# The first eleven Strassen products of the retention input stage put into a fixed order, with the weight and operand sums rearranged to match

## The chip, the cores and the metric

The kernel runs on one NeuronCore of one Trainium2 chip. The metric is the device time of one execution in microseconds, the median of several. The five engines run their own instruction lists and meet at semaphores: TensorE (PE, with weight loads listed apart as PEld), VectorE (DVE), ScalarE (ACT), GpSimd (POOL) and SyncE (SP), whose queue issues most of the DMAs.

## The reference, cut to what matters

One step of a two-layer encoder trunk over 1024 prompt frames and 32 sample frames (T = 1056 columns in all, feature dimension D = 1024), in fp32. The part that the change touches is the input of the first layer, the retention mixer:

```python
h = rmsnorm(x, norm_mix[0])
proj = h @ w_in                     # w_in: 1024 x (2*1024 + 2*2048)
q, k, v, g = jnp.split(proj, [RET_QK, 2 * RET_QK, 2 * RET_QK + RET_V], axis=-1)
# q and k are rotated (rotary), g goes through silu, v into the recurrence
```

The kernel reaches nearly fp32 precision out of fast matmuls: each operand is split into a high part (a cast, on ACT) and a low part (operand minus high part, on DVE), and one product is the sum of high x high, high x low and low x high.

## The kernel before, in words

`ret_in` (line 799) makes q, k and the gates g of the retention layer. The 1056 columns are cut into four quarters c = 0 to 3 of TH = 264. It has two stages.

**The opening.** Head 0's q and k are made in the plain way: `plain(j, c, ds)` (line 918) runs 24 matmuls for each 128 rows (j = 0 is q, j = 1 is k, `ds` are its two row blocks) on quarter c, and a copy on ACT brings the result from PSUM to `qk0`. Quarters 0 and 1 run on operands that aren't normalised yet (`loose`, line 863). Meanwhile `root` (line 886) makes the norms' square roots, `row` (line 898) spreads them along the columns with three small matmuls and a copy, and `parts(c, after)` (line 911) scales a quarter of x, splits it in four pairs (`pair`, line 841: for c = 1 a scaling on ACT and a multiply on DVE; for the others two scalings on DVE; then the cast on ACT at line 856 and the subtraction on DVE at line 858) and leaves it in `XP`. PE's last plain products, of quarters 2 and 3, cover `parts(3)` and `parts(1)`.

**The products by Strassen's scheme.** All other outputs are made in units of 256 rows (`units`, line 954: gate units "g" and q/k units by turns), and for each half s of the columns (s = 0: quarters 0 and 1, s = 1: quarters 2 and 3) a unit takes seven products in place of eight. `product(f, s, i)` (line 443) is the i-th product of unit f on half s in the order `ORD` = M1, M2, M6, M5, M7, M4, M3; it is four k tiles of three matmuls (lines 459, 463, 464), twelve in all. M1, M6 and M7 share one PSUM bank (M6 adds onto M1), M2 and M4 a second, M5 and M3 a third. `snap` (line 436, the copy of line 438) brings a bank to SBUF on ACT before the next product writes on it, and `put` (line 967, the addition of line 968) makes an output block of 264 columns on DVE from a snapped copy and a bank. There are eight banks in all (line 809).

M1 and M2 need the plain split of the weights `rg` (`wgh`, `wgl`) and plain quarters of x. M6, M5, M7, M4 and M3 need sums: of weights, made from `rg` and `rv` by `weight_steps` (line 355; `wsh`/`wsl`, `wth`/`wtl`, `wv`), and of quarters of x, made by `x_sums` (line 323), each a subtraction of 128x1056 on DVE (line 336; s12, s22, s11, s21 in the change), a cast on ACT (line 331) and a subtraction on DVE (line 332), which together are named x5, x6, x7 and x4 after the product that reads them. X[0]'s operands of M6, M7 and M4 go to the tile `XC`, those of half 1 to `XD`, which takes the memory of the raw quarter 0 when that is done with.

What sets the order: each engine runs its list strictly as the framework's planner wrote it. The planner goes by the order in which the program issues instructions and by its own estimate of when each is ready, so products can be interleaved matmul by matmul. `order(a, b)` (line 75) puts instruction a behind b in the planner's list and adds no semaphore. Before, the order of the products comes from the sorted list `seq` (line 1072), which only sets in what order they are issued. The unit's weights are loaded by SP's queue (line 371), the first ones behind the last constant (`normed`, line 1055). On DVE the first gate split and the sums all come behind the last subtraction of `parts(1)` (`held_back`, line 1063).

Of the kernel before, what the change touches and what calls it, by code (L numbers as in the profile page):

```python
# [10 lines left out]
F32 = mybir.dt.float32  # L11
# [7 lines left out]
D = 1024  # L19
# [32 lines left out]
def trunk_kernel(ctx: ExitStack, tc: tile.TileContext, io):  # L52
# [295 lines left out]
    def seven(X, wsrc, sm, snap_room, begin, put, first):  # L348
        W, unit = {}, {}
# [85 lines left out]

        def snap(b):
            t = snap_room()
            ins = S.copy(t, b)  # L438
            if snap_after[0] is not None:
                order(ins, snap_after[0])  # L440
            return t

        def product(f, s, i, after):
# [42 lines left out]
        return weight_sums, product, weight_steps  # L486
# [312 lines left out]
    def ret_in(XP, qk_tile, cs, decays):  # L799
# [41 lines left out]
        def pair(kt, c, after):  # L841
# [44 lines left out]
        def root(c, xms=None, behind=None):  # L886
# [8 lines left out]
            V.tensor_scalar(m_, m_, 1.0 / D, EPS, op0=ALU.mult, op1=ALU.add)  # L895
            rsqrt(r_, t_, m_)

# [13 lines left out]
        def parts(c, after):  # L911
            for kt in range(0, KT, 2):
                end = pair(kt, c, after)
            return end
# [3 lines left out]
        def plain(j, c, ds=(0, 1), after=None):  # L918

            for d in ds:  # L920
# [14 lines left out]
                else:  # L935
                    order(S.copy(qk0[c][:, j, d], ps), last_r[0] or loosened[0])
# [57 lines left out]
        weight_sums, product, weight_steps = seven(X, wsrc, sm, lambda: room("sn"), begin, put, {})  # L994
# [47 lines left out]
        root(3, None, last_r[0])  # L1042
# [18 lines left out]
        first_sums = sums(0)  # L1061
        start = first_sums[0]
        first_sums[0] = lambda: held_back(start(), end[1])
        weight_sums(0, None, first_sums)
        for f in last:
            f()
        for f in sums(1):
            order(f(), x_end[0])
# [3 lines left out]
        seq = [(9.15 if k == 6 else k if k < 9 else max(k, 11 + 0.78 * (k - 9)), 0, k) for k in range(n)]  # L1072
        seq += [(max(k + 3.5, 8.5 + 0.6 * k), 1, k) for k in range(n)]
        for _, s, k in sorted(seq):
            f, i = divmod(k, 7)
            if s == 0 and i == 2 and f == 0:
                second = weight_steps(1, None, None, True)
                next(second)
            elif s == 0 and i == 2 and f + 1 < len(units):
# [1177 lines left out]
    def ffn_up(l, X, fc, sm, he, ready):  # L2257
# [25 lines left out]
        weight_sums, product, weight_steps = seven(X, lambda f: (io["w_up"][l, f], io["w_up"][l, NF + f]), sm,  # L2283
# [428 lines left out]
```

## Time and profile before

| what | value |
|---|---|
| median of 3 runs | 2736.07 us (2733.41 to 2737.28) |
| profiled execution, its own time | 2735.83 us |
| its span, first to last instruction | 2733.8 us |
| PE, DVE, ACT, POOL busy | 99%, 75%, 51%, 15% of the span |
| mean granted clock of PE | 0.997 of full speed |

The change works in the first 110 us of the span, mostly between 38 and 90 us. Times below are microseconds from the span's start unless marked ns. A row of the timeline gives the start, the length, the engine, the source line, the operation with output and inputs, the shapes, and in brackets how long the engine had been idle and what ended that. Neighbouring instructions overlap by some tens of nanoseconds, so the step from one start to the next is what an instruction costs in a full list.

### The profile page before, as it was taken

The numbers are of one execution on the slowest core, as the hardware profiler recorded it, in microseconds if no ns is written. First come the engines' busy times: TensorE is split into PE (matmuls) and PEld (weight loads), VectorE is DVE, ScalarE is ACT, GpSimd is POOL, SyncE is SP. The second block draws the span as 40 slices with busy tenths as digits, with TensorE's granted clock in tenths as the row PEclk, the third lists the DMA queues.
The fourth block names the chain that finished last, engine by engine and source line by source line (L and its number), as shares of the span: only waits on it lengthen the run. The fifth ranks groups of instructions, "written<-read, shape, count | busy, mean of one in ns | idle before, by whom it ended". The sixth has DMA issues, their size and how long they took to land. (4 is left out here: it accounts for less than half of the span.)

```text
span 2733.8 us, 55846 instructions
## 1 busy us (share of the span) xinstructions
PE 2713.2 (99%) x22416; PEld 2624.8 (96%) x22416; DVE 2055.0 (75%) x3645; ACT 1385.3 (51%) x2601; POOL 408.6 (15%) x671
## 2 busy tenths in 40 slices
PE   9999999999999999999999999999999999999998
PEld 9999987778999999999999999999999999999998
DVE  7876667776556988888876788785479888888766
ACT  7544354544345544444544567774355444446445
POOL 0000000000112211111221233320132111112113
PEclk9999999999999999999999999999999999999999
DMA  6233355544876234223888611116533433329884
GB/s 240 92 110 110 114 168 154 158 136 115 277 246 237 99 130 153 96 91 110 271 229 212 185 48 54 54 55 207 190 124 99 147 134 103 106 87 289 233 213 124
DMA packets 278307, 410.18 MB, mean 150 GB/s; under 512 B 57040, under 2 KB 206944, under 8 KB 273952
## 3 DMA queue, kind: packets, MB, share of 16 engines
q1 hardware_dynamic: 259616, 348.23, 38.9%
q0 software_dynamic: 18144, 57.85, 9.0%
q8 instruction: 175, 2.87, 0.4%
q14 instruction: 84, 0.69, 0.1%
q10 hardware_dynamic: 288, 0.54, 0.1%
HBM read 264.34 MB, written 142.21 MB: 149 GB/s over the span
## 5 line engine op out<-in xcount | busy, mean ns | idle before, releaser
L438 ACT COPY HR<-pu 128x264 f32<-128x264 f32 x264 | 98.6, 374 | 265.2 <-PE pu L464 259.5
L459 PE MATMUL pu<-XA,wgh 128*128 128x264 f32 x752 | 213.6, 284 | 0.1
L464 PE MATMUL pu<-XA,wgl 128*128 128x264 f32 x752 | 213.6, 284 | 0.0
L463 PE MATMUL pu<-XA,wgh 128*128 128x264 f32 x752 | 213.3, 284 | 0.0
L2294 DVE SCALAR_TENSOR_TENSOR AR<-AR,cw 128x1058 f32<-128x1058 f32 x88 | 116.0, 1320 | 71.5 <-ACT AR L2293 66.8
L2267 DVE TENSOR_TENSOR AR<-HR,pu 128x264 f32<-128x264 f32 (+2 forms) x440 | 144.7, 371 | 5.3 <-ACT HR L438 3.3
L459 PEld LDWEIGHTS pu<-XA,wgh 128*128 128x128 f32 x752 | 141.9, 189 | 0.4 <-ACT wgh L391 0.4
L463 PEld LDWEIGHTS pu<-XA,wgh 128*128 128x128 f32 x752 | 141.9, 189 | 0.0
L464 PEld LDWEIGHTS pu<-XA,wgl 128*128 128x128 f32 x752 | 141.5, 188 | 0.0
L2291 POOL COPY cst<-AR 128x2 f32<-128x2 f32 x88 | 51.4, 585 | 562.4 <-DVE AR L2267 562.4
L459 PE MATMUL pu<-XA,wth 128*128 128x264 f32 x464 | 132.3, 285 | 2.8 <-ACT wth L391 2.8
L459 PE MATMUL pu<-XA,wsh 128*128 128x264 f32 x464 | 132.2, 285 | 1.0 <-ACT HR L438 0.2
L464 PE MATMUL pu<-XA,wtl 128*128 128x264 f32 x464 | 132.4, 285 | 0.0
L464 PE MATMUL pu<-XA,wsl 128*128 128x264 f32 x464 | 131.8, 284 | 0.0
L463 PE MATMUL pu<-XA,wth 128*128 128x264 f32 x464 | 131.7, 284 | 0.0
L463 PE MATMUL pu<-XA,wsh 128*128 128x264 f32 x464 | 131.4, 283 | 0.0
L2295 DVE SCALAR_TENSOR_TENSOR AR<-AR,cw 128x1058 f32<-128x1058 f32 x88 | 115.9, 1319 | 0.0
L2293 ACT ACTIVATE AR<-AR,cw 128x1058 f32<-128x1058 f32 x88 | 111.8, 1272 | 7.5 <-DVE AR L2267 6.4
L392 DVE TENSOR_TENSOR wtl<-rv,wth 128x1024 fp32r<-128x1024 f32 x58 | 71.0, 1224 | 44.8 <-ACT wth L391 44.7
L391 ACT CAST wgh<-rg 128x1024 fp32r<-128x1024 f32 x58 | 61.0, 1051 | 81.1 <-PE pu L464 77.1
L464 PE MATMUL pu<-XB,wtl 128*128 128x264 f32 x352 | 100.5, 285 | 0.0
L459 PE MATMUL pu<-XB,wth 128*128 128x264 f32 x352 | 99.8, 284 | 0.0
(697 smaller groups left out, 11042.0 us busy)
## 6 DMA issues: line engine op xcount, KB each, us to landing
scr_h<-AR SPq DMA_DIRECT2D x162, 264.0 KB, 2.6
scr_x<-AR POOLq DMA_DIRECT2D x88, 264.0 KB, 6.8
rg<-w_up SPq DMA_DIRECT2D x44, 512.0 KB, 3.6
rv<-w_up SPq DMA_DIRECT2D x44, 512.0 KB, 3.3
raw<-w_ro SPq DMA_DIRECT2D x39, 512.0 KB, 5.0
XA<-scr_h SPq DMA_DIRECT2D x64, 264.0 KB, 4.6
scr_hr<-hl SPq DMA_DIRECT2D x20, 512.0 KB, 3.7
XB<-scr_h SPq DMA_DIRECT2D x34, 264.0 KB, 6.3
```

The source lines that it names most:

```text
L391: cast[0] = split_cast[0] = S.copy(h, src)
L392: split_end[0] = split_last[0] = V.tensor_tensor(l_, src, h.bitcast(F32), op=ALU.subtract)
L438: ins = S.copy(t, b)
L459: mm = PE.matmul(ps, wh[:, k], x[:, 0, kt], start=m in (1, 2, 4, 5) and kt == 0, stop=False, skip_group_check=True)
L463: PE.matmul(ps, wh[:, k], x[:, 1, kt], start=False, stop=False, skip_group_check=True)
L464: mm = PE.matmul(ps, wl[:, k], x[:, 0, kt], start=False, stop=kt == 3, skip_group_check=True)
L2267: last_put[0] = V.tensor_tensor(u[:, d:d + n], t[:, o:o + n], b[:, o:o + n], op=op)
L2291: G.tensor_copy(cst[:, nt, 0:2], uj[:, TP:TP + 2])
L2293: S.activation(cj, uj[:, 2:T + 4], AF.Identity, scale=cw[:, nt, 2:3], bias=cw[:, nt, 3:4])
L2294: V.scalar_tensor_tensor(cj, uj[:, 1:T + 3], cw[:, nt, 1:2], cj, op0=ALU.mult, op1=ALU.add)
L2295: V.scalar_tensor_tensor(cj, uj[:, 0:T + 2], cw[:, nt, 0:1], cj, op0=ALU.mult, op1=ALU.add)
```

## The change

A new generator `first_steps` makes the weights of the first gate unit in place of `weight_steps`. It adds the halves of `rv` behind the `tensor_scalar` of `root(3)`; it splits `rg` in two halves of 512 columns, among the pairs of `parts(3)`, into the third section of `XC` (where x4 of half 0 will lie) and not into weight tiles; and after the last pair of `parts(1)` it chains DVE's work in one order: s12, s22, three halves and `wv`, x5, x6, the `wt` and the `ws` split, then the second unit's `wg` split, s11, s21, x7. The copy of M1 is ordered behind the cast of x7, and x4 behind the output sum of M2 and its cast behind that copy.

The first eleven products are chained on PE: M1 and M2 of half 0, M1 and M2 of half 1, M5 of half 0, M1 of the second unit (half 0), M6, M2 of the second unit (half 0), M7, M4 and M3 of half 0. The snaps of M1 and the output sums of M2 for the first unit's half 1 and the second unit's half 0 are kept (`later`) until the sums of half 1 that read the memory they write are made; those sums are placed one by one behind output sums (`sum_on`, with `puts_after` and `behind`). The scalings of quarter 1 on ACT (`scaled`) are ordered behind casts of quarter 3, and the copies of head 0's k for quarter 2 behind quarter 3's last cast (`ready`). The snap copies of the four first products get their places in a set order. Core of the diff:

```diff
@@ seven @@
-    def seven(X, wsrc, sm, snap_room, begin, put, first):
-        W, unit = {}, {}
+    def seven(X, wsrc, sm, snap_room, begin, put, first, later=()):
+        W, unit, snap_last = {}, {}, [None]
...
+        def first_steps(home, loaded):
+            rg, rv = raw_tile(f"rg{uid()}"), raw_tile(f"rv{uid()}")
+            for r, s_ in zip((rg, rv), wsrc(0)):
+                order(nc.sync.dma_start(r, s_), loaded)
+            a, b = slice(0, 512), slice(512, 1024)
+            h, l_ = home[:, :D], home[:, D:2 * D]
+            W[0] = {1: (h[:, a], l_[:, a]), 2: (h[:, b], l_[:, b])}
+            behind = yield
+            order(V.tensor_tensor(rv[:, a], rv[:, a], rv[:, b], op=ALU.add), behind)
+            for at in (a, b):
+                behind = yield
+                order(S.copy(h[:, at], rg[:, at]), behind[0])
+                order(V.tensor_tensor(l_[:, at], rg[:, at], h[:, at].bitcast(F32), op=ALU.subtract), behind[1])
+            end, pieces = yield
+            last_v = [end[1]]
+
+            def then(ins):
+                order(ins, last_v[0])
+                last_v[0] = ins
+                return ins
+
+            v, th, tl, sh, sl = [w_tile(f"{n}{uid()}") for n in ("wv", "wth", "wtl", "wsh", "wsl")]
+            s12, s22, x6, x5, s11, x7, s21, x4 = pieces
+            then(s12())
+            then(s22())
+            then(V.tensor_tensor(rg[:, a], rv[:, a], rg[:, a], op=ALU.subtract))
+            then(V.tensor_tensor(rg[:, b], rg[:, b], rg[:, a], op=ALU.subtract))
+            order(S.copy(v[:, a], rv[:, b]), end[0])
+            then(V.tensor_tensor(v[:, b], rv[:, b], v[:, a].bitcast(F32), op=ALU.subtract))
+            then(V.tensor_tensor(rv[:, b], rv[:, b], rg[:, a], op=ALU.subtract))
+            then(x5())
+            then(x6())
+            for hh, ll, r in ((th, tl, rv), (sh, sl, rg)):
+                last_r[0] = S.copy(hh, r)
+                wsl_last[0] = then(V.tensor_tensor(ll, r, hh.bitcast(F32), op=ALU.subtract))
...
+            last_v[0] = yield
+            for f in (s11, s21, x7):
+                x_end[0] = then(f())
+            snap_after[0] = x_cast[0]
+            yield
+            x_end[0] = x4()
+            order(x_end[0], puts[-1])
+            order(x_cast[0], snap_last[0])
+            snap_after[0] = None
+            yield
@@ product @@
             if m == 1:
-                d[1] = snap(ps)
+                if not f or (f, s) not in later:
+                    d[1] = snap(ps)
             elif m == 2:
-                put(f, 0, s, 0, ALU.add, d[1], ps)
+                def now(m1=d["a"][:, :TH]):
+                    if 1 not in d:
+                        d[1] = snap(m1)
+                    put(f, 0, s, 0, ALU.add, d[1], ps)
+
+                if (f, s) in later:
+                    later[f, s] = now
+                else:
+                    now()
@@ ret_in @@
-                    order(S.activation(a[:, k], a[:, k], AF.Copy, scale=g), after[0])
+                    order(S.activation(a[:, k], a[:, k], AF.Copy, scale=g), scaled)
...
-                    order(S.copy(qk0[c][:, j, d], ps), last_r[0] or loosened[0])
+                    order(S.copy(qk0[c][:, j, d], ps), ready or last_r[0] or loosened[0])
...
+        later = {(0, 1): None, (1, 0): None}
...
-        root(3, None, last_r[0])
+        third = root(3, None, last_r[0])
...
+        weights0 = first_steps(XC[:, 16 * TH:], asked[0])
+        next(weights0)
+        weights0.send(third)
         end = parts(0, (last_r[0], end[1]))
         mm, _ = row(1, plain(0, 2, (0,), mm))
-        mm, _ = row(3, plain(0, 2, (1,), mm))
-        end = parts(3, end)
-        end = parts(1, end)
+        mm, copied = row(3, plain(0, 2, (1,), mm))
+        ends = []
+        end = parts(3, end, ends)
+        weights0.send((copied, ends[0][1]))
+        weights0.send((ends[0][0], ends[1][1]))
+        end = parts(1, end, scaled=[ends[n][0] for n in (1, 2, 3, 3)])
...
-        plain(1, 2, after=mm)
-        normed[:] = *end, asked[0]
+        plain(1, 2, after=mm, ready=ends[3][0])
...
-        weight_sums(0, None, first_sums)
+        weights0.send((end, sums(0)))
+        second = weight_steps(1, None, None, True)
+        next(second)
+        weights0.send(split_last[0])
...
-        seq = [(9.15 if k == 6 else k if k < 9 else max(k, 11 + 0.78 * (k - 9)), 0, k) for k in range(n)]
+        sooner = {(0, 3): 1.6, (0, 7): 1.8, (0, 8): 2.2, (1, 0): 1.2, (1, 1): 1.4}
+        seq = [(k if k < 9 else max(k, 11 + 0.78 * (k - 9)), 0, k) for k in range(n)]
         seq += [(max(k + 3.5, 8.5 + 0.6 * k), 1, k) for k in range(n)]
+        seq = [(sooner.get((s, k), at), s, k) for at, s, k in seq]
+        behind[0, 1] = x_end[0]
+        chained = [(s, k) for _, s, k in sorted(seq)[:11]]
+        mm = None
...
-            product(f, s, i, None)
+            done = product(f, s, i, mm)
+            mm = done if (s, k) in chained else None
             if (f, s, i) == (0, 1, 1):
+                next(weights0)
+            if (f, s, i) == (1, 0, 1):
+                behind[0, 4] = sum_on(2, x_end[0])
+            if (f, s) == (0, 0) and i in (4, 5):
+                behind[0, i + 1] = sum_on(i - 3, puts[-1])
+            if (f, s, i) == (0, 0, 6):
+                for n, u in ((1, (0, 1)), (2, (1, 0))):
+                    behind[1, 4] = puts_after[0] = sum_on(n, puts[-1])
+                    later[u]()
                 next(second)
-                behind[0, 6] = behind[1, 4] = split_last[0]
```

## Rows read from the trace of the kernel before

**Rows 1.** The page: span, and the first engine's busy time, share and instructions.
```profile
span 2733.8 us, 55846 instructions
## 1 busy us (share of the span) xinstructions
PE 2713.2 (99%) x22416; PEld 2624.8 (96%) x22416; DVE 2055.0 (75%) x3645; ACT 1385.3 (51%) x2601; POOL 408.6 (15%) x671
```

**Rows 2.** The waits of PE from 0 to 300 us: total, times, longest.
```profile
PE pu L459 <- ACT wth L391: 2.8, 1, 2.8
...
PE pn L903 <- DVE rr L194: 0.5, 1, 0.5
```

**Rows 3.** Busy time by stretch, with PE's granted clock (PEclk).
```profile
core 0: us, PE busy (x) PEld busy (x) DVE busy (x) ACT busy (x) POOL busy (x), PEclk, DMA share, GB/s
20.00:40.00 20.00, 19.54 (x156) 18.91 (x155) 11.56 (x37) 14.28 (x36) 0.00 (x0) 1.00 0.88 346
...
62.64:65.43 2.79, 0.00 (x0) 0.00 (x1) 2.75 (x5) 1.10 (x2) 0.00 (x0) 0.85 0.03 6
65.43:71.38 5.95, 5.81 (x24) 5.51 (x25) 5.95 (x7) 3.32 (x4) 0.00 (x0) 0.50 0.51 176
71.38:73.38 2.00, 2.00 (x18) 2.00 (x18) 2.00 (x2) 0.00 (x0) 0.00 (x0) 0.99 0.00 0
```

**Rows 4.** PE's timeline, first and last matmul of M1 and M2, and M5's first.
```profile
59.58 0.28 PE L459 MATMUL pu<-XA,wgh 128*128 128x264 f32 x1
...
62.36 0.28 PE L464 MATMUL pu<-XA,wgl 128*128 128x264 f32 x1
65.43 0.59 PE L459 MATMUL pu<-XA,wth 128*128 128x264 f32 x1 [2.79 <-ACT wth L391]
```

**Rows 5.** DVE's timeline from 38 to 56 us.
```profile
39.01 0.16 DVE L192 TENSOR_TENSOR rr<-rr 128x2 f32<-128x2 f32 x1 [0.93 <-ACT rr L190]
...
42.54 1.71 DVE L850 SCALAR_TENSOR_TENSOR ARi<-ARi,gcol,R 128x264 f32<-128x264 f32 x4 [0.16 <-ACT R L906]
...
46.19 0.71 DVE L858 TENSOR_TENSOR XA<-ARi,XA 128x528 fp32r<-128x528 f32 x1 [0.92 <-ACT XA L856]
...
48.65 0.68 DVE L407 TENSOR_TENSOR rv<-rv 128x512 f32<-128x512 f32 x1
...
51.66 1.33 DVE L858 TENSOR_TENSOR XA<-ARi,XA 128x528 fp32r<-128x528 f32 x2 [0.22 <-ACT XA L856]
...
55.74 1.25 DVE L336 TENSOR_TENSOR ARi<-ARi,sp 128x1056 f32<-128x1056 f32 x1
```

**Rows 6.** DVE's timeline from 63 to 99 us.
```profile
63.61 0.69 DVE L424 TENSOR_TENSOR rv<-rv,rg 128x512 f32<-128x512 f32 x1
...
73.53 0.43 DVE L968 TENSOR_TENSOR ARi<-ARi,pu 128x264 f32<-128x264 f32 x1
73.87 1.25 DVE L336 TENSOR_TENSOR ARi<-ARi 128x1056 f32<-128x1056 f32 x1
...
76.83 1.25 DVE L336 TENSOR_TENSOR ARi<-ARi 128x1056 f32<-128x1056 f32 x1
78.00 1.25 DVE L332 TENSOR_TENSOR XD<-ARi,XD 128x1056 fp32r<-128x1056 f32 x1
...
87.84 1.23 DVE L392 TENSOR_TENSOR wsl<-rg,wsh 128x1024 fp32r<-128x1024 f32 x1 [0.52 <-ACT wsh L391]
88.98 0.69 DVE L423 TENSOR_TENSOR wv<-rv,wv 128x512 fp32r<-128x512 f32 x1
...
97.43 0.69 DVE L423 TENSOR_TENSOR wv<-rv,wv 128x512 fp32r<-128x512 f32 x1
98.03 0.68 DVE L411 TENSOR_TENSOR rg<-rg 128x512 f32<-128x512 f32 x1
```

**Rows 7.** ACT's timeline from 61 to 70 us.
```profile
61.61 0.62 ACT L422 CAST wv<-rv 128x512 fp32r<-128x512 f32 x1
64.33 1.05 ACT L391 CAST wth<-rv 128x1024 fp32r<-128x1024 f32 x1 [2.10 <-DVE rv L424]
...
69.99 0.37 ACT L438 COPY ARi<-pu 128x264 f32<-128x264 f32 x1
```

**Rows 8.** The tile `rv` up to 112 us: its loads (the first at 28.3).
```profile
L371 SPq DMA_DIRECT2D rv<-w_rg x3: 333/412/527, 28.3 to 102.5; - x3
...
DMA to landing us min/median/max: 3.2/3.5/9.2
```

**Rows 9.** Busy time by stretch further on, with PE's granted clock.
```profile
1620.00:1630.00 10.00, 7.85 (x55) 7.31 (x55) 7.36 (x28) 8.49 (x35) 5.30 (x10) 0.89 0.00 0
1630.00:1640.00 10.00, 10.00 (x69) 10.00 (x68) 9.97 (x25) 7.20 (x18) 0.13 (x1) 0.94 0.39 144
```

More of the change, by code (lines that the diff above doesn't have):

```diff
@@ L434, in weight_steps @@
             W[f].update({5: (s1[0][:, a], s1[1][:, a]), 7: (s1[0][:, b], s1[1][:, b])})
+        def first_steps(home, loaded):
[31 more added lines that the diff above has]
+                wsl_last[0] = then(V.tensor_tensor(ll, r, hh.bitcast(F32), op=ALU.subtract))
+            W[0].update({6: (sh[:, a], sl[:, a]), 3: (sh[:, b], sl[:, b]), 4: (v[:, a], v[:, b]),
+                         5: (th[:, a], tl[:, a]), 7: (th[:, b], tl[:, b])})
+            last_v[0] = yield
[8 more added lines that the diff above has]
+            yield
         def snap(b):
@@ L440, in snap @@
                 order(ins, snap_after[0])
+            snap_last[0] = ins
             return t
@@ L484, in product @@
             return mm
-        return weight_sums, product, weight_steps
+        return weight_sums, product, weight_steps, first_steps
     scr_og = io["scr_og"]
@@ L839, in ret_in, with pair @@
         w0 = {}
-        def pair(kt, c, after):
+        def pair(kt, c, after, scaled):
             a = xr[c][:, kt:kt + 2]
@@ L894, in root @@
             m_, t_, r_ = [rr[:, k, j0:j0 + n] for k in range(3)]
-            V.tensor_scalar(m_, m_, 1.0 / D, EPS, op0=ALU.mult, op1=ALU.add)
+            ins = V.tensor_scalar(m_, m_, 1.0 / D, EPS, op0=ALU.mult, op1=ALU.add)
             rsqrt(r_, t_, m_)
+            return ins
         def row(c, after):
@@ L909, in row, with parts, plain @@
             return mm, copied
-        def parts(c, after):
+        def parts(c, after, ends=None, scaled=(None,) * 4):
             for kt in range(0, KT, 2):
-                end = pair(kt, c, after)
+                end = pair(kt, c, after, scaled[kt // 2])
+                if ends is not None:
+                    ends.append(end)
             return end
         qk0 = [qk_tile() for _ in range(4)]
-        def plain(j, c, ds=(0, 1), after=None):
+        def plain(j, c, ds=(0, 1), after=None, ready=None):
             for d in ds:
@@ L992, in refill @@
             nc.gpsimd.dma_start(XP[:, 2 * s + 1, 0], io["scr_x5"][s])
-        weight_sums, product, weight_steps = seven(X, wsrc, sm, lambda: room("sn"), begin, put, {})
+        later = {(0, 1): None, (1, 0): None}
+        snaps = [room("sn") for _ in range(4)]
+        snaps = [snaps[i] for i in (0, 3, 1, 2)]
+        weight_sums, product, weight_steps, first_steps = seven(
+            X, wsrc, sm, lambda: snaps.pop(0) if snaps else room("sn"), begin, put, {}, later)
         V.memset(rr, 1.0)
@@ L1060, in ret_in, with sum_on @@
         more(1, es.enter_context(pool("xd", side="right")).tile([P, 24 * TH], F32R, tag="XD", name="XD"))
-        first_sums = sums(0)
-        start = first_sums[0]
-        first_sums[0] = lambda: held_back(start(), end[1])
-        weight_sums(0, None, first_sums)
+        weights0.send((end, sums(0)))
+        second = weight_steps(1, None, None, True)
+        next(second)
+        weights0.send(split_last[0])
         for f in last:
             f()
-        for f in sums(1):
-            order(f(), x_end[0])
+        x_rest = sums(1)
+        def sum_on(n, after):
+            for _ in range(n):
+                ins = x_rest.pop(0)()
+                order(ins, after)
+                after = ins
+            return ins
         turns = [(c, j) for c in range(4) for j in range(2)]
         n = 7 * len(units)
-        seq = [(9.15 if k == 6 else k if k < 9 else max(k, 11 + 0.78 * (k - 9)), 0, k) for k in range(n)]
+        sooner = {(0, 3): 1.6, (0, 7): 1.8, (0, 8): 2.2, (1, 0): 1.2, (1, 1): 1.4}
+        seq = [(k if k < 9 else max(k, 11 + 0.78 * (k - 9)), 0, k) for k in range(n)]
         seq += [(max(k + 3.5, 8.5 + 0.6 * k), 1, k) for k in range(n)]
+        seq = [(sooner.get((s, k), at), s, k) for at, s, k in seq]
+        behind[0, 1] = x_end[0]
+        chained = [(s, k) for _, s, k in sorted(seq)[:11]]
+        mm = None
         for _, s, k in sorted(seq):
             f, i = divmod(k, 7)
[L1076 to L1079, printed above, removed]
+            if s == 0 and i == 2 and 0 < f < len(units) - 1:
                 weight_sums(f + 1)
@@ L2281, in edges @@
                     order(k, joined[0])
-        weight_sums, product, weight_steps = seven(X, lambda f: (io["w_up"][l, f], io["w_up"][l, NF + f]), sm,
+        weight_sums, product, weight_steps, _ = seven(X, lambda f: (io["w_up"][l, f], io["w_up"][l, NF + f]), sm,
                                      lambda: room("sn"), begin, put, FIRST)
```

## The prediction

> **What bounds the kernel now.** The page comes first: TensorE (PE) is busy for 2713.2 of 2733.8 us [rows 1], so a gain can only be a PE gap that closes, and an operation added on another engine costs only where PE comes to wait for it. The profiled execution took 2735.83 us, 0.24 below the median of the three runs, 2736.07; the sum goes against the first, and 0.24 is added at the end.
>
> Next the waits of PE in the first 300 us: one large one, 2.8 us, in front of a product of the first gate unit, ended by ScalarE's cast `wth` on line 391 [rows 2]. The windows show what it costs beyond itself [rows 3]. In the wait (62.64 to 65.43) no matmul runs. Behind it, from 65.43 to 71.38, the granted clock is 0.50, the 1.2 GHz level, and 24 matmuls take the place of some 49; from 71.38 on it is 0.99, the 2.4 GHz level. A shorter wait of 0.5 us [rows 2], in the stretch from 20 to 40, left the clock there at 1.00 [rows 3]. So the gap costs 2.79 us of idle time and 5.95 x 0.50 = 2.97 us of clock: **5.76 us**, 0.21% of the run. A measurement of this kernel can tell 0.2%, 5.5 us here, from no change, so the whole prize is about that size.
>
> Why PE waits: a product is twelve matmuls. M1 and M2 of the first half start 59.58 to 62.36, 23 steps of 0.121 us [rows 4], so a product takes 1.45 us. The third product, M5, needs `wth`. That cast starts at 64.33, when VectorE (DVE) has made `rv` (63.61 plus 0.69) [rows 6, 7]. DVE is the cause: it began the chain of sums at 55.74 [rows 5] and is busy for 2.75 of the 2.79 us of the wait [rows 3].
>
> **What the change removes.** Four products that need nothing of that chain (M1 and M2 of both halves) now stand in front of M5, so PE asks for `wth` and `wtl` at 59.58 + 4 x 1.45 = 65.38. Call T0 the start of the first sum on DVE (55.74 before). The start-to-start costs are 1.17 us for 1056 columns (76.83 to 78.00), 1.14 for 1024 (87.84 to 88.98), 0.60 for 512 (97.43 to 98.03), 0.34 for an output sum of 264 (73.53 to 73.87) [rows 6]. In the new chain `wtl` is done after two sums of 1056, four halves, two splits of 1056 and one of 1024: 2.34 + 2.40 + 2.34 + 1.14 = 8.22 us after T0, 0.09 later with its tail. Before PE asks there is 65.38 - 8.3 = 57.1 for T0. I take it that the gap goes: minus 5.76.
>
> **T0 in the new order.** Before, DVE's stretch from 42.54 to 55.74 (13.20 us) holds the parts of c=3 and c=1, the addition in `rv` at 48.65 (0.60) and idle spells of 0.92 and 0.22 us [rows 5]. The addition now goes behind `root(3)`, where DVE sits idle for 0.93 us ahead of 39.01 [rows 5]; it fits, if its load has landed: issue at 28.3, at most 9.2 us to landing [rows 8], 37.5 us, just before. The first gate split goes ahead of T0 as two halves of 0.60 on DVE, in place of one of 1.14 behind it. So T0 = 42.54 + 13.20 - 0.60 + 1.20 = 56.34 if the idle spells stay, and 55.20 if they close. That DVE waited there for ScalarE's casts, and that the change moves ScalarE's scalings of c=1 up into its pauses and the k copies back behind the casts, speaks for the lower end. I take 55.3, and keep both for the range.
>
> Here a rule speaks against the change. The rows say that a 1024-column split costs 1.14 and two halves 1.20 from start to start, 0.06 us more [rows 6]. The Trainium skill ("VectorE: DVE Perf Modes", the section on the TRN2 errata) says that operands in SBUF pay a fixed latency per instruction, so that few large tiles beat many small ones. By its formula for fp32, (N+151)/0.96 ns, an estimate, two halves would cost 0.16 us more, and T0 and the sum would be 0.1 us later. The trace agrees in sign, and lets neighbours overlap.
>
> **What new waits stand where.** (a) M6, the seventh product, writes over M1's bank, so it waits for the copy of M1, which is now ordered behind ScalarE's cast of x7, which waits for DVE's s11. That is 9.36 (the chain to `wsl`) + 1.14 (`wgl` of the second unit) + 1.17 + 0.08 = 11.75 us after T0; then the cast, about 1.0, and the copy, 0.37 [rows 7], with 0.05 of signalling: T0 + 13.2, so 68.4 to 69.5. PE is there at 59.58 + 6 x 1.45 = 68.28. The eleven are chained, so nothing fills this wait: 0.1 to 1.3 us; I take 0.2. (b) M3 needs M7's output sum, which is behind x7, one output sum, x4 and two sums: T0 + 10.5 + 3.51 + 0.34 + 3.51 + 0.42 = T0 + 18.3, 73.5 to 74.6, against 59.58 + 10 x 1.45 = 74.1: nothing at the lower end, 0.5 at the upper. x4 itself, moved behind M1 and M2 of both halves because the weights now lie in its place, is done at T0 + 15.6, 71 to 72, and M4 asks at 72.6: nothing. (c) The second unit's `ws` split. DVE must first do nine sums or splits of 1056, six output sums and three halves behind x7's split: T0 + 14.0 + 10.5 + 2.0 + 1.8 = T0 + 28.3; with the cast and split (1.05 + 1.23 + 0.1) T0 + 30.7, so 85.9 to 87.0. Without it PE has 7 + 7 products of the first unit and four (M1, M2, both halves) of the second: 18 x 1.45 = 26.1, to 85.7. Before, it ended at 87.84 + 1.23 = 89.07 [rows 6]. So 0.2 to 1.3 here. These three are not added: a wait at (a) moves PE, and so its later demands, by as much, and what is lost in all is the largest of them, 0.2 to 1.3 us. At T0 = 55.3 that is (c) with 0.3; I take 0.4, for the signalling that I haven't counted.
>
> **What costs nothing.** ScalarE's extra half cast (0.62 us for 512 columns [rows 7]) goes into its pauses. No DMA is added; the two weight loads keep their place behind the last constant on SP's queue, and POOL's queue isn't touched. The k copies hold two PSUM banks some 1 to 4 us longer, which the new products don't ask for before 59.58; if that cover went, each would cost PE the copy's wait, under 1 us. Two products of M1 and M2 keep their banks until their output sums, at about 82 us; with them the eleven use seven of the eight banks.
>
> The sum: -5.76 + 0.4 = -5.36; 2735.83 - 5.36 = 2730.47, and with 0.24, **2730.7 us**. Nothing after 90 us changes in amount, PE is full, and I carry the gain to the end. By the bounds of T0 the gain lies between 5.6 and 4.5.
>
> **Rivals.** (1) **DVE becomes the bound**: from T0 to the end of the second unit's `wsl` it takes as long as before, 89.07 - 55.74 = 33.3 us, because output sums and rotations get in between; then `wsl` comes at 88.6 and PE has waited 2.9 us by then, in pieces short enough to leave the clock alone as the 0.5 us one did: 2736.07 - 5.76 + 2.9 = 2733.2. For it: DVE was busy all through the wait [rows 3]. Against: a split of 1.14 and a cast's wait are gone from that stretch. (2) **The gap only moves**: M6 waits for the copy as long as M5 did for the cast, 2.8 us or so, with the same clock loss; T0 would have to be 57.9. Then nothing is gained, 2736. The change then doesn't do what it says. For it: the copy is behind more DVE work than `wth` was. Against: there are three more products of cover. (3) **Slower**: the same lateness strikes twice, in front of M6 and again at the second unit's weights, each with 2.8 us idle and 2.97 us of the 1.2 GHz level, 11.5 against 5.76 removed: 2736.07 + 5.8 = 2741.9. It decides from T0 = 57.9 on, if PE then has no other product to put in at (c). For it: PE runs in the order given. The Trainium skill ("TensorE: Matmul & The Clock Gate", "Step-by-step: what each phase is for") has matmuls in program order with only weight loads pulled ahead; the trace agrees, since M1 and M2 of the second half were ready and PE still idled for 2.79 us. (4) **A dip elsewhere goes or comes**: at 1620 to 1640 us the granted clock is 0.89 and 0.94 [rows 9], which is 1.1 + 0.6 = 1.7 us lost; work that arrives 5 us sooner may meet no dip there: 2730.7 - 1.7 = 2729.0.
>
> **How the numbers follow.** The forecast has 0.60, rival 1 0.12, rival 2 0.06, rival 3 0.11, rival 4 0.11. The forecast's own range is 2729.2 to 2732.6: T0's bounds (2730.5 to 2731.6), and on either side about 1 us of the 1 to 3 us by which the runs shown stand from their median. The bound of 0.2% is 2730.6, just inside it: half of the forecast and rival 4 are past it, 0.30 + 0.11 = 0.41 for faster. The rest of the forecast with rivals 1 and 2 makes 0.48 for the same, rival 3 0.11 for slower. The range leaves out rival 3 and the far end of rival 4: 2728.0 to 2737.0.
>
> **What would show it.** Right: no wait of PE over 1 us between 55 and 95 us, granted clock 1.00 in all of it, the product M5 of the first half at about 65.4, the eleventh product done near 75.5 and the weights `wsl` of the second unit near 86. Wrong: a wait of PE for a copy on line 438's place or for `wsh`/`wsl`, a stretch at 0.50 after it, or the start of the first sum on DVE later than 57 us. If the first 100 us come out as said and the end doesn't, the gain was lost later, and the waits behind 112 us have to be compared.

## The result and the profile after

The changed kernel takes 2740.55 us (median of 18 runs, 2738.91 to 2743.39), the kernel before 2735.61 us in the same series (18 runs, 2733.11 to 2738.93). The ratio is 1.0018, interval [1.0011, 1.0026]: **slower by 3 to 7 us**, where the prediction had 2730.7 us and a range of 2728.0 to 2737.0. The middle of the interval is just under the 0.2% that the prediction took as the smallest change to be told; the whole interval lies above 1. In the series of the experiments one execution of run 2 took 6783.83 us, and its median and ratio are given without that one. All profile lines below that name no kernel are of the changed one; its profiled execution has a span of 2737.9 us, 4.1 more than before.

The page, span and first busy times, answers to [rows 1]:

```profile
span 2737.9 us, 55848 instructions
## 1 busy us (share of the span) xinstructions
PE 2714.0 (99%) x22416; PEld 2623.9 (96%) x22416; DVE 2054.3 (75%) x3646; ACT 1385.4 (51%) x2602; POOL 401.8 (15%) x671
```

DVE's amount of work is the same to a microsecond. What changed is who waits for whom. The waits of PE from 0 to 300 us answer to [rows 2]:

```profile
PE pu L508 <- ACT XD L331: 2.1, 2, 1.4
PE pu L512 <- DVE XD L332: 1.8, 2, 0.9
PE pu L508 <- ACT ARi L486: 1.1, 1, 1.1
...
PE pn L962 <- DVE rr L194: 0.5, 1, 0.5
```

The wait for `wth` is gone. In its place stand 1.1 us for the copy of M1 (M6 waits for it) and 3.9 us for the high and low parts in `XD`, the operands of half 1. The same stretch by windows answers to [rows 3] (PE, PEld, DVE, ACT, POOL busy, then the granted clock):

```profile
59.90:65.77 5.87, 5.87 (x51) 5.87 (x49) 5.83 (x7) 3.33 (x4) 0.00 (x0) 1.00 0.01 3
65.77:69.99 4.22, 3.09 (x27) 2.88 (x25) 4.22 (x5) 1.51 (x3) 0.00 (x0) 1.00 0.75 248
69.99:81.23 11.24, 10.57 (x84) 10.35 (x84) 9.43 (x12) 5.74 (x9) 0.00 (x0) 1.00 0.00 0
81.23:87.39 6.16, 2.91 (x17) 2.30 (x18) 4.69 (x6) 1.35 (x2) 0.00 (x0) 1.00 0.01 3
87.39:90.80 3.41, 3.41 (x18) 3.41 (x18) 2.23 (x5) 1.24 (x2) 0.00 (x0) 0.50 0.00 0
```

The first two windows are what was forecast: no idle time up to M5, DVE full (5.83 of 5.87, 4.22 of 4.22). In the fourth PE works less than half of the time, and in the fifth, behind it, the granted clock is at 0.50, the 1.2 GHz level. PE's timeline gives the price of each wait; M5's first row answers to the last of [rows 4]:

```profile
65.77 0.28 PE L508 MATMUL pu<-XA,wth 128*128 128x264 f32 x1
...
68.58 0.28 PE L513 MATMUL pu<-XA,wgl 128*128 128x264 f32 x1
69.99 0.39 PE L508 MATMUL pu<-XC,wsh 128*128 128x264 f32 x1 [1.13 <-ACT ARi L486]
70.22 0.29 PE L512 MATMUL pu<-XC,wsh 128*128 128x264 f32 x1
...
80.28 0.28 PE L513 MATMUL pu<-XA,wtl 128*128 128x264 f32 x1
81.23 0.39 PE L508 MATMUL pu<-XD,wth 128*128 128x264 f32 x1 [0.67 <-ACT XD L331]
82.52 0.39 PE L512 MATMUL pu<-XD,wth 128*128 128x264 f32 x1 [0.90 <-DVE XD L332]
...
83.84 0.28 PE L513 MATMUL pu<-XD,wtl 128*128 128x264 f32 x1
85.56 0.39 PE L508 MATMUL pu<-XD,wv 128*128 128x264 f32 x1 [1.44 <-ACT XD L331]
86.85 0.39 PE L512 MATMUL pu<-XD,wv 128*128 128x264 f32 x1 [0.91 <-DVE XD L332]
```

From start to start, with 0.12 us for a matmul taken off, M6 loses (69.99 - 68.58) - 0.12 = 1.29 and 0.11 in the next step; M7 of half 1 loses 0.83 + 1.17 + 0.11; M4 of half 1 loses 1.60 + 1.17 + 0.11. Together 6.4 us, and, counted as the prediction counts the clock, 3.41 x 0.5 = 1.7 us: 8.1. The gap before cost 65.43 - 62.36 - 0.12 = 2.95 [rows 4] and 2.97 of clock: 5.9. So the stage loses 2.2 us; 0.3 more was lost by 59 us (the first M1 starts at 59.90, not 59.58), a part that differs from execution to execution (0.2 in the changed kernel's second profiled execution). At 130 us PE's list is 2.6 us later than before. Another 1.1 us comes between 2440 and 2590 us (told below).

Why half 1's operands are late stands in DVE's timeline, which answers to [rows 5] and [rows 6]:

```profile
45.09 0.69 DVE L444 TENSOR_TENSOR rv<-rv 128x512 f32<-128x512 f32 x1
...
55.54 0.71 DVE L916 TENSOR_TENSOR XA<-ARi,XA 128x528 fp32r<-128x528 f32 x1 [0.75 <-ACT XA L914]
56.16 1.25 DVE L336 TENSOR_TENSOR ARi<-ARi,sp 128x1056 f32<-128x1056 f32 x1
...
81.21 1.26 DVE L332 TENSOR_TENSOR XD<-ARi,XD 128x1056 fp32r<-128x1056 f32 x1 [0.80 <-ACT XD L331]
82.50 0.43 DVE L1029 TENSOR_TENSOR ARi<-ARi,pu 128x264 f32<-128x264 f32 x1
82.85 1.25 DVE L336 TENSOR_TENSOR ARi<-ARi 128x1056 f32<-128x1056 f32 x1
85.54 1.26 DVE L332 TENSOR_TENSOR XD<-ARi,XD 128x1056 fp32r<-128x1056 f32 x1 [1.44 <-ACT XD L331]
...
90.64 1.23 DVE L392 TENSOR_TENSOR wsl<-rg,wsh 128x1024 fp32r<-128x1024 f32 x1 [1.11 <-ACT wsh L391]
```

and in ACT's, which answers to [rows 7]:

```profile
69.56 0.66 ACT L486 COPY ARi<-pu 128x264 f32<-128x264 f32 x2 [0.17 <-DVE sp L336]
...
80.11 1.07 ACT L331 CAST XD<-ARi 128x1056 fp32r<-128x1056 f32 x1 [0.45 <-DVE ARi L336]
84.16 0.38 ACT L486 COPY ARi<-pu 128x264 f32<-128x264 f32 x1 [2.98 <-PE pu L513]
84.43 1.07 ACT L331 CAST XD<-ARi 128x1056 fp32r<-128x1056 f32 x1
```

The new order puts the sums of half 1 one by one behind output sums. DVE makes s11, then waits 0.80 us for the cast of x7, subtracts (81.21), adds an output block (82.50), and only then makes s21 (82.85 to 84.10). Its cast stands on ACT behind a copy that itself waited 2.98 us for PE (84.16), which puts it back by another 0.27 us at most. Before, s21 (by the program's order the last of the four sums) stood ahead of the subtraction of x7, so that the cast of x7 (ACT, 78.98 to 80.07) ran beside it. DVE's timeline of the kernel before:

```profile
79.17 1.25 DVE L336 TENSOR_TENSOR ARi<-ARi 128x1056 f32<-128x1056 f32 x1
80.33 1.25 DVE L332 TENSOR_TENSOR XD<-ARi,XD 128x1056 fp32r<-128x1056 f32 x1
```

After the change DVE idles here although it is the engine that everything waits for.

### The profile page after: what moved, and what is told of

It reads as the page before. It is cut to its first block, busy times and chain, and to the rows that moved or that the text cites. A ratio compares the mean times of both kernels' runs of the same rounds, so it can differ in the third digit from the quotient of the medians.

```text
span 2737.9 us, 55848 instructions
## 1 busy us (share of the span) xinstructions
PE 2714.0 (99%) x22416; PEld 2623.9 (96%) x22416; DVE 2054.3 (75%) x3646; ACT 1385.4 (51%) x2602; POOL 401.8 (15%) x671
## 5 line engine op out<-in xcount | busy, mean ns | idle before, releaser
L508 PE MATMUL pu<-XA,wgh 128*128 128x264 f32 x736 | 208.2, 283 | 0.0
L512 PE MATMUL pu<-XA,wgh 128*128 128x264 f32 x736 | 208.1, 283 | 0.0
L508 PEld LDWEIGHTS pu<-XA,wgh 128*128 128x128 f32 x736 | 138.2, 188 | 0.0
L512 PEld LDWEIGHTS pu<-XA,wgh 128*128 128x128 f32 x736 | 138.2, 188 | 0.0
```

Of the source, the lines that this page charges most:

```text
L508: mm = PE.matmul(ps, wh[:, k], x[:, 0, kt], start=m in (1, 2, 4, 5) and kt == 0, stop=False, skip_group_check=True)
L512: PE.matmul(ps, wh[:, k], x[:, 1, kt], start=False, stop=False, skip_group_check=True)
```

## The experiments

All times are medians of 10 or more runs beside the kernel before in the same series (2735.7 to 2736.4 us), except in runs 10 and 11, one profiled execution each. The ratios are to the kernel before. The changed kernel's 2740.55 us comes from another series, whose kernel before took 2735.61, so a difference to it can be off by the 0.1 to 0.8 us between the series.

The runs of one kernel spread by some us, so a second measure, one trace for each kernel, stands beside the medians: the time between the starts of the 429th and the 962nd matmul of PE's list (59.09 and 130.11 us in the kernel before), less the same time in the kernel before. It leaves out the opening and all that comes later.

| trace | PE's loss (+) or gain (-) from 59 to 130 us |
|---|---|
| changed kernel, first and second profiled execution | +2.2, +2.3 |
| kernel before, second profiled execution | -0.6 |
| runs 1, 2, 3, 4 | -0.1, -0.1, -1.2, +2.5 |
| runs 5, 6 | +2.2, +4.8 |
| runs 7, 8, 9 | -2.3, -4.4, -3.8 |

**1. The order of half 1's sums alone.** s21 goes right behind s11:

```diff
         x_rest = sums(1)
+        x_rest[5], x_rest[6] = x_rest[6], x_rest[5]
...
-                for n, u in ((1, (0, 1)), (2, (1, 0))):
+                for n, u in ((2, (0, 1)), (1, (1, 0))):
```

> The changed kernel with the half 1 difference s21 made directly behind s11, ahead of the split of x7, and x4's split alone behind x7's output sum. Theory A (the loss comes from the sums of half 1 made in series: DVE makes s21 only behind x7's split and an output sum, so the cast of x4 starts late and DVE and PE both wait): the two waits in front of M4 of half 1 (1.44 and 0.91 us) go, the half-clock stretch at 87 to 91 us goes with them, the waits in front of M7 of half 1 (0.67 and 0.90) stay; 3.5 to 4.5 us faster than the changed kernel, about the time of the kernel before. Theory B (the fixed order of products as such loses it): M4's waits only shrink by the 1.2 us that one difference takes, the stretch at half clock stays, under 1.5 us gained. Theory C (the loss is in the stage at 2450 to 2560 us, where the DMA engines are full): the first 130 us win, and the end doesn't.

Measured: 2737.04 us, ratio to before 1.0004 [0.9996, 1.0013]: 3.5 us faster than the changed kernel. M4's two waits and the stretch at half clock are gone; 1.1 us remain at M6, 0.7 and 1.2 at M7, 0.7 and 0.2 at the second unit's `wsh` and `wsl`. Theory A. So that order is what made the change worse than the kernel before, but without it nothing is won either.

**2. More work for PE instead.** M1 and M2 of the second unit's half 1, which need nothing late, go in front of M7 of half 1:

```diff
-        later = {(0, 1): None, (1, 0): None}
+        later = {(0, 1): None, (1, 0): None, (1, 1): None}
-        sooner = {(0, 3): 1.6, (0, 7): 1.8, (0, 8): 2.2, (1, 0): 1.2, (1, 1): 1.4}
+        sooner = {(0, 3): 1.6, (0, 7): 1.8, (0, 8): 2.2, (1, 0): 1.2, (1, 1): 1.4, (1, 7): 10.5, (1, 8): 10.6}
-        chained = [(s, k) for _, s, k in sorted(seq)[:11]]
+        chained = [(s, k) for _, s, k in sorted(seq)[:16]]
...
+                later[1, 1]()
```

> The changed kernel with M1 and M2 of the second unit's half 1 put into the fixed order ahead of M7 of half 1 (their copy and output sum come later). Nothing on DVE or ACT is made sooner; PE only gets 2.9 us more of work in front of the late operands. Theory A: M7's waits (1.6 us) go and M4's (2.35 us) shrink to some 1 to 2 us, and what PE saves there is asked back in part at the second unit's ws weights near 91 us, since DVE is as late as it was: 0 to 3 us faster than the changed kernel. Theory B: 4 us or more faster, because only the order was wrong.

Measured: 2736.98 us, 1.0006 [0.9997, 1.0015], 3.6 us faster than the changed kernel: just past A's end and short of B's. M7's waits are gone and M4's are 0.3 and 0.9 us; 0.7, 0.2 and 0.5 us stand at the second unit's weights. DVE is as late as it was (its waits of 0.81 and 1.14 us for casts of `XD` and of 1.11 for `wsh` are there), but PE has 2.9 us of work to put in.

**3. Only the gap, in the kernel before.** M1 and M2 of half 1 are issued behind those of half 0, the rest stays:

```diff
+        seq = [({(1, 0): 1.2, (1, 1): 1.4}.get((s, k), at), s, k) for at, s, k in seq]
-            if (f, s, i) == (0, 1, 1):
+            if (f, s, i) == (1, 0, 1):
```

> The kernel before with one edit: M1 and M2 of half 1 are issued right behind M1 and M2 of half 0, with the second unit's weight step hung on the second unit's M2. No chain on PE, no other order on DVE. Theory A (the four products in front cover the late wth cast; what the change lost came from its own order of half 1's sums): the 2.79 us wait and the half-clock stretch behind it go or shrink to under 1 us, and the kernel is 2 to 5 us faster than before. Theory B (four products ahead aren't enough, because DVE can't feed PE in the next 30 us whatever the order): the waits come back between 75 and 95 us, within 1.5 us of before.

Measured: 2735.41 us, 0.9998 [0.9990, 1.0007]. The wait for `wth` and the half clock are both gone, and the time stays. PE's timeline, the rows with a wait between 59 and 95 us:

```profile
66.73 0.39 PE L459 MATMUL pu<-XA,wgh 128*128 128x264 f32 x1 [0.44 <-ACT wgh L391]
...
70.52 0.39 PE L464 MATMUL pu<-XA,wgl 128*128 128x264 f32 x1 [1.75 <-DVE wgl L392]
...
81.59 0.39 PE L459 MATMUL pu<-XD,wth 128*128 128x264 f32 x1 [0.81 <-ACT ARi L438]
...
86.64 0.39 PE L459 MATMUL pu<-XA,wsh 128*128 128x264 f32 x1 [0.36 <-DVE ARi L968]
```

The 5.9 us of the gap come back as 0.8 us at 160 us, or 1.2 counted from 59 us on. Theory B in the time; two of the four waits come ahead of the 75 us that it named. Where PE comes sooner, it waits again: twice for DVE's own result, and twice for a cast or a copy on ACT.

**4. Without the chain on PE.** The changed kernel with the eleven products linked by data alone:

```diff
-            mm = done if (s, k) in chained else None
+            mm = None
```

> The changed kernel without the links that chain the first eleven products on PE; the planner may interleave them, all else stays. Theory A: no great change, because the waits are behind the eleven, in products that weren't chained: within 1.5 us of the changed kernel, the waits in front of M7 and M4 of half 1 still there; the wait of 1.13 us in front of M6 may be filled. Theory B: the waits are filled with other products and 3 us or more come back.

Measured: 2740.15 us, 1.0018 [1.0009, 1.0027], as the changed kernel: theory A. M6 doesn't wait any more, but two new waits stand behind it, at M7 of half 0 and at M6 of half 1:

```profile
72.80 0.39 PE L508 MATMUL pu<-XC,wth 128*128 128x264 f32 x1 [0.35 <-ACT ARi L486]
...
78.23 0.39 PE L512 MATMUL pu<-XD,wsh 128*128 128x264 f32 x1 [0.30 <-DVE XD L332]
```

The waits at M7 and M4 of half 1 are as they were (0.68, 0.90, 1.44 and 0.91 us), with half clock behind them (88.42 to 91.83). The chain isn't the cause.

**5 and 6. DVE's work as such.** If DVE is the bound, work added to it must show in full, in the kernel *before*: the work goes behind the gap, where PE didn't wait. The low parts of x7 and x4 of half 0 are subtracted twice (and in run 6 also those of x6 and x5 of half 1); the second subtraction writes the same values:

```diff
+                for _ in range(2 if doubled and (doubled[0], o) in ((0, 7), (0, 4)) else 1):
+                    ins = V.tensor_tensor(X[o][:, 1], v, X[o][:, 0].bitcast(F32), op=ALU.subtract)
+                return ins
-                return V.tensor_tensor(X[o][:, 1], v, X[o][:, 0].bitcast(F32), op=ALU.subtract)
```

> The kernel before with two subtractions on VectorE done twice (the low parts of x7 and of x4, half 0): 2 x 1.17 = 2.34 us of VectorE work more behind the gap, nothing else changed. Theory A (VectorE's list between 55 and 92 us is the bound of that stretch, so that whatever the matmul order gains is asked back there): the time rises by 1.5 to 5 us, with the upper end if the new waits take the clock down; the waits of TensorE at M7, M4 or the second unit's ws weights grow by about 2 us. Rival B (VectorE has slack behind the gap, and the change lost only by the order of its list): at most 0.7 us more, since the 2.3 us go into VectorE's idle spells (4.3 us between 40 and 110 us).

> The kernel before with four subtractions on VectorE done twice (low parts of x7 and x4 of half 0 and of x6 and x5 of half 1): 4 x 1.17 = 4.68 us of VectorE work more behind the gap. Theory A (VectorE is the bound there): 2 to 4 us more than the run with two of them doubled, 4 to 9 us over the kernel before. Rival B (slack): at most 2 us over the kernel before.

Measured: 2738.74 us (1.0014 [1.0005, 1.0022]) and 2742.17 us (1.0022 [1.0013, 1.0032]): +2.95 us for 2.34 us of DVE work and +6.4 for 4.68. By the intervals these are 1.4 to 6.0 and 3.6 to 8.8 us. From 59 to 130 us the traces lose 2.2 and 4.8 us, about one for one; in run 6 a wait of 3.2 us for a low part (83.20) and a second stretch at a lower clock (0.84 and 0.82 between 80 and 90 us) are in it. Theory A in both. PE's timeline of run 5, rows with a wait (a wait of 0.44 us for `wgh` right behind the first is left out):

```profile
65.61 0.39 PE L463 MATMUL pu<-XA,wth 128*128 128x264 f32 x1 [2.80 <-ACT wth L395]
...
82.29 0.39 PE L467 MATMUL pu<-XD,wsh 128*128 128x264 f32 x1 [0.56 <-DVE XD L335]
84.84 0.39 PE L463 MATMUL pu<-XD,wth 128*128 128x264 f32 x1 [0.95 <-ACT ARi L442]
89.88 0.39 PE L463 MATMUL pu<-XA,wsh 128*128 128x264 f32 x1 [0.41 <-DVE ARi L980]
```

The last three aren't in the kernel before. There PE just didn't wait behind the gap: 5.9 us later, it met operands that were just ready. That is why the page's 75% for DVE says nothing here; it is the windows of this stretch that say it.

**7. Both repairs together** (the edits of 1 and 2).

> The changed kernel with both repairs: s21 of half 1 made right behind s11 (x7 before x4 without an output sum between), and M1 and M2 of the second unit's half 1 put in front of M7 of half 1. Each alone was 3.3 to 3.5 us faster than the changed kernel (2740.5). Theory A (both take away the same loss, and what is left is the second unit's weights behind VectorE): 2735.5 to 2737.5, waits left at M6 (1.1) and at the second unit's weights. Rival B (the two repair different waits): the gains add up, 2733 to 2734.5, and the waits at x7, x4 and at the weights are all gone.

Measured: 2734.77 us, 0.9997 [0.9989, 1.0006]: 5.8 us below the changed kernel and within the noise of the kernel before, between A and B in time; the waits left are A's (M6 1.1, the second unit's weights 0.5, 0.4 and 0.2).

**8. And DVE's pauses at the second unit's weights filled.** In `weight_steps` the halves of `wv` and `rv` come ahead of the `ws` split, so that DVE has work while ACT casts:

```diff
             v = tile("wv")
+            hold(S.copy(v[:, a], rv[:, b]), 1)
+            V.tensor_tensor(v[:, b], rv[:, b], v[:, a].bitcast(F32), op=ALU.subtract)
+            ins = V.tensor_tensor(rv[:, b], rv[:, b], rg[:, a], op=ALU.subtract)
+            x_steps(1, ins)
             if mixed is not None or late is True:
                 s2 = split(rg, "ws")
...
-            hold(S.copy(v[:, a], rv[:, b]), 1)
-            V.tensor_tensor(v[:, b], rv[:, b], v[:, a].bitcast(F32), op=ALU.subtract)
-            ins = V.tensor_tensor(rv[:, b], rv[:, b], rg[:, a], op=ALU.subtract)
-            x_steps(1, ins)
```

> The changed kernel with both repairs and, in the second unit's weights, the halves of v and rv put ahead of the ws split, so that VectorE has other work while ScalarE casts wsh and wth (it idled 1.11 and 1.12 us there in the changed kernel). Theory A (VectorE's list is the bound, its idle spells are the loss): 1 to 2.5 us below the run with both repairs alone, wtl of the second unit done 2 us sooner, and faster than the kernel before by 1 to 3 us. Rival B (TensorE is held by M6 and by later stages): within 0.7 us of the run with both repairs.

Measured: **2732.58 us, 0.9988 [0.9979, 0.9997]**: 3.2 us below the kernel before (0.8 to 5.7 by the interval) and 8 below the changed one. Theory A: 2.2 us less than run 7. Its window of 75 to 95 us, and its only wait of PE between 40 and 130 us:

```profile
75.00:95.00 20.00, 20.00 (x165) 19.87 (x164) 18.62 (x27) 12.07 (x18) 0.00 (x0) 1.00 0.18 61
```

```profile
PE pu L508 <- ACT ARi L486: 1.3, 1, 1.3
```

PE is full there at 1.00; in the changed kernel it works 16.08 of those 20 us. This version beats both kernels, by about 0.1% the kernel before. Of the 4.4 us that it gains from 59 to 130 us, 1.3 are lost again between 2440 and 2590 us.

**9. T0 made earlier.** On top of run 8, quarter 1's four multiplications stand ahead of its four subtractions on DVE, so that the pause of 0.75 us ahead of the first sum goes:

```diff
+            if c == 1:
+                whole = [halfway(kt, c, after, scaled[kt // 2]) for kt in range(0, KT, 2)]
+                for kt, a in zip(range(0, KT, 2), whole):
+                    end = split(kt, c, after, a, whole[-1][1])
+                return end
```

(`halfway` is `pair`'s scaling and multiplication, `split` its cast and subtraction.)

> The kernel with both repairs and the new weights order (2732.6), with quarter 1's parts made in two passes on VectorE: all four multiplications first, then all four subtractions, so that VectorE doesn't wait 0.75 us for ScalarE's last cast before the first sum (56.44 there). Theory A (VectorE's list is the bound up to M6, the only wait of TensorE left there, 1.26 us): T0 at 55.5 to 55.8, the wait at M6 shrinks to about 0.6, the time to 2731.5 to 2732.2, 0.4 to 1 us less. Rival B (M6's wait comes from ScalarE or from the copy's own place, not from VectorE): the wait stays over 1 us and the time within 0.3 us.

Measured: 2732.92 us, 0.9987 [0.9978, 0.9996], the same as run 8, and the wait at M6 is 1.6 us: rival B. The first sum starts at 55.37, but the pause comes back later; ACT's and DVE's timelines:

```profile
60.16 0.38 ACT L1018 COPY qk<-pj 128x264 f32<-128x264 f32 x1 [1.13 <-PE pj L1012]
60.43 1.08 ACT L331 CAST XA<-ARi 128x1056 fp32r<-128x1056 f32 x1
```

```profile
61.54 1.26 DVE L332 TENSOR_TENSOR XA<-ARi,XA 128x1056 fp32r<-128x1056 f32 x1 [0.97 <-ACT XA L331]
```

The cast of x5 now stands on ACT behind a copy of k, which waits for PE's last plain product. A chain of DVE that passes through casts is only as early as the casts' places in ACT's list.

**10 and 11. Second executions.** The changed kernel and the kernel before, unchanged, profiled once more.

> The changed kernel as it is, a second profiled execution: which part of its loss belongs to the kernel and which to one execution. Theory A (the loss is made between 66 and 92 us, and what comes at 2440 to 2560 us, where the DMA share is 0.96 and more, varies from execution to execution): the waits at M6, M7, M4 and the stretch at half clock near 88 us are there again within 0.3 us, the wait of 0.55 us at 2546 us is not, or has another size. Rival B (the change moves the late stage too): the wait at 2546 us is there again with the same size.

> The kernel before as it is, a second profiled execution, as a ruler for the late stage: the wait for wth (2.8 us) and the half clock behind it again within 0.3 us. Between 2440 and 2560 us TensorE's waits differ from those of the first profile by up to 1 us if that stage varies by itself (theory A), and agree within 0.2 us if it doesn't (rival B).

They took 2738.66 and 2735.68 us. The waits between 60 and 92 us are there again (2.1, 1.6 and 1.1 us after; before 2.8, and 0.4 more for `wgh`); the stretches at half clock have other lengths, against what was expected of both (last section). The late wait is there again too: 0.6 us the first time, 0.7 the second, for a sum (`AR`) at about 2546 us, where the DMA share is about 0.9 and DVE has waited 3.8 and 3.9 us for a load of `w_down`, against 2.2 and 3.4 before. Windows of that stretch, of the kernel before, the first and the second execution:

```profile
2530.00:2560.00 30.00, 30.00 (x249) 30.00 (x248) 20.90 (x35) 13.69 (x25) 3.46 (x4) 1.00 0.89 246
```

```profile
2530.00:2560.00 30.00, 29.90 (x245) 29.69 (x244) 20.69 (x36) 13.73 (x25) 3.47 (x4) 1.00 0.89 242
```

and of the changed kernel:

```profile
2530.00:2560.00 30.00, 29.45 (x242) 29.24 (x241) 21.60 (x36) 12.95 (x23) 5.19 (x6) 1.00 0.91 242
```

```profile
2530.00:2560.00 30.00, 29.34 (x240) 29.13 (x240) 19.05 (x32) 12.05 (x21) 4.33 (x5) 1.00 0.89 238
```

PE loses 0.6 us in the changed kernel both times and 0 to 0.1 before. That is rival B's sign, but the other traces speak against a property of the change: runs 1, 2 and 4, which are small variants of the changed kernel, lose at most 0.1 us there, run 3, a variant of the kernel before, loses 1.1 (28.87 us busy), and runs 8 and 9, which arrive sooner, 0.6 and 0.4. What moves that load isn't settled; no run tried it.

## Why the prediction was wrong, point by point

**The gap goes: right, its price only partly.** M5 starts at 65.77, without a wait, where 65.4 was forecast. The 2.79 us of idle time stand in both executions of the kernel before. The 2.97 us of clock don't: in the second the stretch at 0.50 is 3.41 us long, not 5.95, 1.7 us of loss by the same count. By the table above PE's work from 59 to 130 us took 0.6 us less there, so 5.76 was the price of one execution.

**T0: forecast 55.3, measured 56.16**, near the upper bound, 56.34. The addition in `rv` did not go into the pause ahead of 39.33 but among the parts of c=3 (45.09). Its load had landed (issued at 29.0, 9.0 us to landing, so 38.0); the likely reason, which no run tried, is the planner's list: `order` only says behind what an instruction comes. The pauses of 0.92 and 0.22 us did close, but one of 0.75 us opened ahead of the last subtraction (55.54), and DVE's stretch began 0.3 us later (42.84).

**(a) M6: the wait is inside its bounds, in part by luck.** With T0 at 56.16 the formula T0 + 13.2 gives 69.4 for the end of the copy, and a wait of 1.1 us against 68.28; 1.13 was measured, where 0.1 to 1.3 was allowed and 0.2 taken. But the copy starts at 69.56, so it ends 0.6 us later than that: the cast began 0.4 us late (68.31), and the copy waited 0.17 us more for s21, which wasn't in the formula. PE too was 0.4 us later (68.70), and the two nearly cancel. **(b) M3 and M4 of half 0**: nothing, as forecast.

**(c) is the step that failed.** "T0 + 30.7" counts DVE's instructions end to end. With T0 measured it gives 86.9 for the end of the second unit's `wsl`; it came at 90.64 + 1.23 = 91.87, 5.0 us later. Of these 3.1 are pauses of DVE for casts of sums of x (0.21, 0.63, 0.80, 1.44), none of which was in the sum; the pause of 1.11 for `wsh` was in it, as the cast's 1.05. Another 0.4 us was lost ahead of the end of x7's subtraction of half 0 (70.59, where T0 + 14.0 gives 70.16), and seven output sums stood in the stretch, not six (0.34). The rest is steps longer than the start-to-start costs. And the sum asked only when the *weights* are ready. M7 and M4 of half 1, which PE reaches before, weren't looked at, and they are where the time went: 5.0 us from start to start, and the 1.7 us of clock. At the second unit's weights themselves PE didn't wait. The line "what is lost in all is the largest of them, 0.2 to 1.3 us" stands against 6.4 us of waits, and no term for the clock behind them was in the sum.

**One slip of the text ahead of the prediction:** of the first unit's half 1 only M2's output sum is kept back; its copy of M1 is made at once (the condition `not f`). No term of the sum rested on it.

**The rivals.** Rival 1 (DVE is the bound) was the right mechanism with 0.12 and too low a price: it let DVE need the same 33.3 us from T0 to `wsl`, and it needed 35.7; and the waits did take the clock, which it left out. Its argument against ("a split of 1.14 and a cast's wait are gone from that stretch") overlooked that casts' waits came into it elsewhere. Rival 2 was wrong: M6 waited 1.13 us, not 2.8, and the clock stayed at 1.00 behind it. Rival 3 came near the time, 2741.9 against 2740.55, which is luck: the lateness did strike twice, but at M6 with 1.1 us and no loss of clock, and at M7 and M4 of half 1, not at the weights; its condition (T0 from 57.9 on) didn't hold. Rival 4's dip at 1620 to 1640 us goes with the execution and not with the time of arrival: the changed kernel has it in its first (0.83 from 1630 to 1640) and not in its second (1.00), which arrives at the same time and gains 1.1 us on the first between 1500 and 2000 us. The row that should have decided was cited for rival 1: DVE busy 2.75 of 2.79 us in the wait, and 5.95 of 5.95 behind it [rows 3]. Where the feeder's list is full, closing a wait of PE alone gave 1.2 us of the 5.9 (run 3), and work added to the feeder cost about its own length (runs 5 and 6).

The Trainium skill ("Perfetto Trace Analysis", "Optimization Strategy") says that the most-contended engine can change over time, from one regime of a kernel to another, and that the gaps are to be looked for within the regime of interest. The traces agree: PE is busy for 99% of the span, and DVE for 10.05 of 10.09 us between 59.90 and 69.99 us.

## What to carry to other kernels

Before an order of the bottleneck's instructions is changed to close a wait, add up in the windows behind it whether its feeder (the engine that makes its operands) has slack: doubling one harmless instruction of the feeder measures that in one run. Where the feeder was full, two things helped here: work for the bottleneck that needs nothing from the feeder (run 2), and taking away the feeder's own pauses by keeping two independent sums in flight around a cast (runs 1 and 8). And follow every operand of the products that come next, not only the last of the chain.

## What was not expected of the hardware

**A wait costs more than its idle time.** PE's idle rows show 5.05 us (1.13, 0.67, 0.90, 1.44, 0.91), but from start to start 6.4 us are gone, 0.27 more for each: the first matmul behind a wait takes 0.39 us in place of 0.28, and the next starts 0.23 behind it in place of 0.12. Five short waits so cost 1.35 us beyond their idle time. Of each 0.27, 0.16 is only the difference between a matmul's length as the profile models it (0.28) and its step in a full list (0.12), since idle time is counted from the modelled end; the other 0.11 is the longer first matmul (0.39), behind which the next starts late. The Trainium skill ("TensorE: Matmul & The Clock Gate", "Step-by-step: what each phase is for") has the drain of one matmul overlap the fill of the next when they run back to back; by that a wait exposes one drain, and the rows agree in sign; how much of the 0.27 it is, no run shows.

**The stretch at half clock isn't the same each time.** Behind the same waits it took other lengths. The two executions of the kernel before, the first of which is in [rows 3] (5.95 us from the restart on), and here the second, which begins some 2 us behind the restart:

```profile
67.52:70.93 3.41, 3.41 (x18) 3.41 (x17) 3.41 (x4) 2.43 (x3) 0.00 (x0) 0.50 0.45 159
```

and the second execution of the changed kernel, where the first had 87.39 to 90.80:

```profile
83.82:90.65 6.83, 4.68 (x20) 4.13 (x19) 4.14 (x8) 2.48 (x4) 0.00 (x0) 0.50 0.00 0
```

At 0.50 matmuls step by 0.22 us (14 steps from 87.49 to 90.57 in the first execution of the changed kernel) in place of 0.12, so a little under half of the time is lost: 1.5 us of a full 3.41. The stretch of 6.83 us lies in part over waits and holds only 4.68 us of PE's work: from 59 to 130 us the two executions of the changed kernel differ by less than 0.1 us. The two of the kernel before, 5.95 us of it from the restart on against 3.41, differ by 0.6. A sum that takes the clock's price from one profile has that spread in it.
